# Sums of the input made inside the first down group, and a fifth pair of the up projection by seven products

## The chip, the cores and the metric

The kernel runs on one core of one Trainium2 chip. The metric is the device time of one execution in microseconds, as the median of several runs; smaller is better. The chip's matrix engine is called PE in the profile, its vector engine DVE, its scalar engine ACT, its general engine POOL; SP only issues transfers.

## The reference, cut to what matters

The model is a stack of four layers on 512 tokens with 1024 channels. Each layer has a token mixer (layer 0 and 3 a convolution module, layer 1 neighbourhood attention, layer 2 retention) and after it a gated feed-forward block with a short depthwise convolution. Only the feed-forward block, the channel mixer of the layer, is touched here:

```python
def conv_ffn(h, w_up, dw_w, dw_b, w_down):
    u = dwconv(h @ w_up, dw_w, dw_b)
    val, gate = jnp.split(u, 2, axis=-1)
    return (jax.nn.gelu(gate) * val) @ w_down

for i in range(DEPTH):
    ...
    h = rmsnorm(x, norm2_g[i])
    x = x + conv_ffn(h, ffn_w_up[i], ffn_dw_w[i], ffn_dw_b[i], ffn_w_down[i]).astype(x.dtype)
```

FFN_DIM is 2816, so the up projection has 44 column tiles of 128: 22 of values and 22 of gates. All is float32.

## The kernel before

Everything is kept transposed: a tile has 128 channels as partitions and 512 tokens as columns. Every float32 operand is split into a high and a low part (a cast on ACT makes the high part, a subtraction on DVE the low one), and a product of two such operands takes three matmuls (`mm3`, L184 to L187): high by high, high by low, low by high.

**The up projection.** Pair j of 22 is the value tile j and the gate tile j. In the plain way (`up`, L307) a tile takes 8 channel blocks by 3 matmuls of 512 columns, 24 in all, so a pair takes 48. For the pairs listed in `UPS` (L78) the pair is made at once by Strassen's scheme in Winograd's form, with seven products in place of eight (`up_macro`, L384): the pair is seen as a 2 by 2 block matrix (two output tiles by two halves of the channels) times a 2 by 2 block matrix (two halves of the channels by two halves of the tokens). A product (`uprod`, L371) is 4 blocks by 3 matmuls of 256 columns, so the pair takes 84 matmuls of 256 columns. Two products per pair are left to the start of the next one (`finish_up`). For this scheme there must be sums of the weight blocks and sums of the input blocks. The weight sums of a pair come from `sums` (L484: SP loads a block, POOL adds another to it by an accumulating transfer, tile tag `ws`, three buffers) and `weights` (L501: splits and two additions, on ACT and DVE).

**The input sums.** `combos(p)`, for p from 0 to 3, makes four sums of 256 columns from the normalized input tiles x[2p] and x[2p+1] with four DVE instructions, writes them into one `ws` buffer, and splits them into `ch` (ACT) and `cl` (DVE). `COMBO` (L79) places the four calls behind pairs 4, 5, 6 and 7. The first pair of `UPS` needs all of them.

**Between the matmuls**, `mid` does the depthwise convolution, the GELU and the product of value and gate for a pair, and the sums of that product for the down projection.

**The down projection.** The first 16 blocks of the hidden width are done in two parts (`PARTS`, L71); part 0 starts behind pair 8 (pair 9 in layer 1), part 1 behind pair 16 (17). `down` (L539) runs four groups i = 0 to 3 in each part, each again by seven products of 4 blocks by 3 matmuls of 256 columns. This is what a group does, in the order of the code:

- `weights(...)` for the group;
- product a11 into one half of a PSUM bank, `xc`; ACT copies it to the right half of the tile `s12` (L559);
- product a22 into `v`; then product s2 on top of a11 in `xc`, so it may begin only when that copy has been read;
- ACT copies `xc` again (L562), then s1 and s3;
- ACT takes `xc` into `u2` (L566), DVE subtracts `v` from it (L568), and POOL adds `u2` to the residual in DRAM, `xd[2i]`, by an accumulating transfer (L569);
- the last two products of the group before (`finish`, L541), a DVE addition into its `s12` (L545), and an accumulating transfer of it to `xd[2i+1]` (L546).

The tiles `s12`, `u2` and the temporaries of `mid` share one tag of seven buffers (`NT_FFN`, L75, `t512`). A buffer is used again when its last reader is through; for `s12` and `u2` of a down group that is the transfer by POOL.

**What sets the order.** Each engine runs its own queue in order. The queues are written by a scheduler that goes by its own estimate of durations and by the order of the code; the engines wait for each other by semaphores. A wait holds up everything that stands behind it on its engine. In the names of the waits, DMASW is a transfer issued by POOL that has landed, DMAHW one issued by SP or ACT.

Of the kernel before, what the change touches and what calls it, by code (L numbers as in the profile page):

```python
# [8 lines left out]
F32 = mybir.dt.float32  # L9
F32R = mybir.dt.float32r  # L10
# [7 lines left out]
P = 128  # L18
T = 512
D = 1024  # L20
KD = D // P
DEPTH = 4
EPS = 1e-6
CW = 31
FT = 22
# [49 lines left out]
NT_FFN = 7  # L75
NWS = 3
SCALED = (5, 7, 5, 5)
UPS = ((10, 11, 18, 19), (11, 12, 18, 19), (10, 11, 18, 19), (10, 11, 18, 19))  # L78
COMBO = (4,5,6,7)  # L79
LATEW = True  # L80
COVER = (0, 0)
L1 = 1
SPILL = 2
# [4 lines left out]
def tile_trunk(  # L88
# [9 lines left out]
    const = ctx.enter_context(tc.tile_pool(name="const", bufs=1))  # L98
# [7 lines left out]
    def nm(s):  # L106
        uid[0] += 1
        return f"{s}{uid[0]}"
# [31 lines left out]
    x = [const.tile([P, T], F32, tag=f"x{k}", name=f"x{k}") for k in range(KD)]  # L140
# [53 lines left out]
    def split(src, hi, lo, n=None):  # L194
        state["cast"] = nc.scalar.copy(hi, src)
        return nc.vector.tensor_tensor(lo, src, hi.bitcast(F32), SUB)
# [42 lines left out]
    @contextmanager  # L239
    def behind(*names):  # L240
        with ExitStack() as st:
            for n in names:
                st.enter_context(tc.issue_after(state[n].ins))
            yield
# [57 lines left out]
    def ffn(l, after):  # L302
        with ExitStack() as st:
            stage_pools(st, NT_FFN, 8, 0)
            hp = st.enter_context(tc.tile_pool(name=nm("ffn"), bufs=1, reuse_waits=RW))
# [39 lines left out]
            ch, cl = {}, {}  # L345

            def combos(p):
                e, o = x[2 * p], x[2 * p + 1]
                c = hp.tile([P, D], F32, tag="ws", name=nm("cx"), bufs=NWS)
                q = [c[:, i * 256:(i + 1) * 256] for i in range(4)]  # L350
                with behind("scaled"):
                    nc.vector.tensor_tensor(q[0], e[:, 256:], e[:, :256], SUB)
                    nc.vector.tensor_tensor(q[1], o[:, :256], e[:, :256], SUB)
                nc.vector.scalar_tensor_tensor(q[2], o[:, :256], -1.0, q[0], MUL, SUB)
                nc.vector.scalar_tensor_tensor(q[3], q[2], -1.0, o[:, 256:], MUL, SUB)
                cl[p] = hp.tile([P, D], F32R, tag=f"cl{p}", name=nm("cl"))
                for k, h in ((2 * p, slice(0, T)), (2 * p + 1, slice(T, D))):
                    ch[k] = const.tile([P, T], F32R, tag=f"x{k}", name=nm("ch"))
                    split(c[:, h], ch[k], cl[p][:, h])

            def xblock(p, b):
                if b in (1, 2, 3):
# [138 lines left out]
            def weights(src, r13, sg, r1, hold=False):  # L501
                n = src.shape[-1] // 4
                if r1 is None:
                    r1 = load_raw(src[:, :2 * n], 2 * n)
                w1 = split_w(r1, 2 * n, nc.vector)
                w13 = (whi.tile([P, D], F32R, tag="wh", name=nm("wh")),
                       wlo.tile([P, D], F32R, tag="wl", name=nm("wl")))
                r2 = r13[:, n:2 * n]
                with behind("Hh") if hold else ExitStack():
                    nc.scalar.copy(w13[0][:, :2 * n], r13[:, :2 * n])  # L510
                with behind("Hl") if hold else ExitStack():
                    nc.vector.tensor_tensor(w13[1][:, :2 * n], r13[:, :2 * n],
                                            w13[0][:, :2 * n].bitcast(F32), SUB)
                nc.vector.tensor_tensor(r2, r2, r1[:, :n], ADD)
                h2 = hp.tile([P, T], F32R, tag="h2", name=nm("h2"))
                l2 = hp.tile([P, T], F32R, tag="l2", name=nm("l2"))
                split(r2, h2[:, :n], l2[:, :n])
                nc.vector.tensor_tensor(sg[:, :n], r2, sg[:, n:2 * n], ADD)
                h4 = hp.tile([P, D], F32R, tag="h4", name=nm("h4"))
                l4 = hp.tile([P, D], F32R, tag="l4", name=nm("l4"))  # L520
                split(sg[:, :2 * n], h4[:, :2 * n], l4[:, :2 * n])
                u = lambda w, b: (w[0][:, b * n:(b + 1) * n], w[1][:, b * n:(b + 1) * n])
                return {"a11": u(w1, 0), "a22": u(w1, 1), "s3": u(w13, 0), "s1": u(w13, 1),
                        "s2": u((h2, l2), 0), "sg": u((h4, l4), 0), "a12": u((h4, l4), 1)}

            def down_sums(i, q):
                p0, p1 = PARTS[q]
                c = PART_COL[q]
                return sums(f_down[l, i][:, c:c + 4 * (p1 - p0) * P], state["load"] if i == 0 else None, i == 0)

            def prod(o, w, q, b, start, stop=True, part=None):
                p0, p1 = PARTS[q]
                for p in part or range(p0, p1):
                    s = slice((p - p0) * P, (p - p0 + 1) * P)
                    hi, lo = H[p]
                    mm3(o, w[0][:, s], w[1][:, s], hi[:, b, :], lo[:, b, :],
                        start and p == p0, stop and p == p1 - 1, True)

            def down(q, first, late, filler):  # L539
                p0, p1 = PARTS[q]  # L540

                def finish(i, w, v, s12):
                    prod(v[:, :256], w["sg"], q, 2, False)
                    prod(v[:, 256:], w["a12"], q, 3, True)
                    nc.vector.tensor_tensor(s12, v, s12, ADD)  # L545
                    nc.gpsimd.dma_start(xd[2 * i + 1], s12, accum_op=ADD)  # L546

                prev = None
                for i in range(4):
                    w = weights(*down_sums(i, q)) if i else first  # L550
                    xb, v = bank(psa), bank(psa)
                    xc = xb[:, :256]
                    s12 = t512()
                    if i == 0:
                        prod(xc, w["a11"], q, 1, True, part=range(p0, p1 - 1))
                        prod(v[:, 256:], w["a22"], q, 6, True, part=range(p0, p1 - 1))
                    now = range(p1 - 1, p1) if i == 0 else None
                    prod(xc, w["a11"], q, 1, True, part=now)
                    nc.scalar.copy(s12[:, 256:], xc)  # L559
                    prod(v[:, 256:], w["a22"], q, 6, True, part=now)  # L560
                    prod(xc, w["s2"], q, 0, False)
                    nc.scalar.copy(s12[:, :256], xc)  # L562
                    prod(v[:, :256], w["s1"], q, 4, True)
                    prod(xc, w["s3"], q, 5, False)
                    u2 = t512()
                    nc.scalar.activation(u2.rearrange("p (h t) -> p h t", h=2),  # L566
                                         xc.unsqueeze(1).broadcast_to([P, 2, 256]), AF.Copy, scale=-1.0)
                    nc.vector.tensor_tensor(u2, u2, v, SUB)  # L568
                    nc.gpsimd.dma_start(xd[2 * i], u2, accum_op=ADD)  # L569
                    if prev:  # L570
                        finish(*prev)
                    prev = (i, w, v, s12)
                late()
                filler()
                finish(*prev)
# [49 lines left out]
            def fetch_sums(j):  # L625
                if j in UPS[l] and j not in ahead:
                    ahead[j] = sums(f_us[l, UPS[l].index(j)], state["load"])

            def ups_of(j):
                nonlocal n  # L630
                fetch_sums(j + 1)
                if j in UPS[l] and n < 2 * j + 2:
                    ups.extend(up_macro(j))
# [5 lines left out]
                for p in range(4):  # L639
                    if COMBO[p] == j:  # L640
                        combos(p)

            starts = {2 * p1 + (l == 1 and q == 0) * L1 + COVER[q]: q for q, (_, p1) in enumerate(PARTS)}
            for j in range(1, FT):
                ups_of(j)
                w0 = down_sums(0, starts[j]) if j in starts else None
                if w0 and not LATEW:
                    w0 = weights(*w0)
                if n > S2[l]:
                    mids(j)  # L650
                if w0 and LATEW:
                    w0 = weights(*w0, True)
# [690 lines left out]
    kind, l = seq[0]  # L1343
# [51 lines left out]
def _layout(inp):  # L1395
    import numpy as np

    f = {k: np.asarray(v) for k, v in inp.items()}
# [12 lines left out]
    par = np.zeros((P, NPAR), np.float32)  # L1411
# [25 lines left out]
    cl = np.arange(16)[:, None, None, None]  # L1437
    kc = np.arange(32)[None, None, :, None]
    masks = []
    for b, ks in ((0, 0), (1, 8), (3, 32)):  # L1440
        c = 16 * b + cl
# [10 lines left out]
    for sh in range(PH):  # L1452
        for r in range(PH):
# [12 lines left out]
    fu = f["ffn_w_up"].reshape(4, 4, 2, P, 44, P)  # L1466
    fus = np.stack([np.stack([np.concatenate(
        [fu[l, :, par, :, j + c].transpose(1, 0, 2).reshape(P, T)
         for c, par in ((0, 0), (FT, 1), (FT, 0), (0, 1))], -1) for j in UPS[l]]) for l in range(DEPTH)])
    fd = f["ffn_w_down"].reshape(4, FT, P, 8, P)  # L1470
    macros = []
    for i in range(4):
# [48 lines left out]
```

## Time and profile before

| what | us |
|---|---|
| median of 3 runs | 2527.53 |
| lowest and highest run | 2527.3 and 2529.24 |
| the profiled execution, whole | 2528.47 |
| its span in the trace | 2526.7 |
| busy in that span: DVE | 1825.3 (72%) |
| busy in that span: ACT | 1267.8 (50%) |
| busy in that span: POOL | 373.0 (15%) |

The profiled execution is 1.77 us longer than its span, and 0.94 us longer than the median of the runs. Starts are counted from the beginning of the span. [...]

### The profile page before, as it was taken

The page shows a single profiled execution, that of the slowest core. Times are in us where ns is not written, and L with a number is a line of the kernel's source. Part 1 is how long each engine was busy: PE and PEld are TensorE (multiplying, and loading weights), DVE is VectorE, ACT ScalarE, POOL GpSimd, SP SyncE. Part 2 cuts the span into 40 slices and gives each one's busy share as a digit, 9 for nine tenths or more (in the row PEclk, how much of TensorE's full clock was granted, in tenths as well). Part 3 has the DMA queues.
Part 4 walks back from the last instruction along what each step waited for, and adds up shares of the span by engine and source line. Part 5 has one row for each costly group of instructions (what it writes and reads, how often), then busy time and mean ns, then how long its engine had stood idle before and what let it go on. Part 6 is the DMA issues. An engine that isn't in the chain of part 4 may idle for free.

```text
span 2526.7 us, 38769 instructions
## 1 busy us (share of the span) xinstructions
PE 2508.2 (99%) x15166; PEld 2170.0 (86%) x15166; DVE 1825.3 (72%) x3021; ACT 1267.8 (50%) x1778; POOL 373.0 (15%) x443
## 2 busy tenths in 40 slices
PE   9999999999999999999999999999999999999999
PEld 7888898989998889898888888889898888789897
DVE  7976867677877786767656566686767887686765
ACT  5454645465656565555332423464545445464543
POOL 2114010103320201120000000201010121201010
PEclk9999999999999999999999999999999999999999
DMA  7736776746653566773222222477664673477664
GB/s 257 227 96 184 192 162 176 164 141 163 141 136 109 138 169 165 195 172 116 75 84 74 83 75 65 145 185 162 175 163 142 206 228 89 121 193 162 177 161 133
DMA packets 130153, 379.22 MB, mean 150 GB/s; under 512 B 15360, under 2 KB 22400, under 8 KB 129968
## 3 DMA queue, kind: packets, MB, share of 16 engines
q1 hardware_dynamic: 90816, 280.45, 35.5%
q0 software_dynamic: 38000, 93.96, 20.1%
q8 instruction: 119, 1.95, 0.3%
q10 hardware_dynamic: 1152, 2.33, 0.3%
q14 instruction: 66, 0.54, 0.1%
HBM read 342.11 MB, written 30.79 MB: 148 GB/s over the span
## 4 chain that ended last, share of the span: by engine, by line
PE 93%; issue 3%; DVE 2%; DMA 1%; ACT 1%; SPq 0%; POOL 0%; DVEq 0%; POOLq 0%; ACTq 0%
PE ps L185 22%; PE ps L186 22%; PE ps L187 22%; PE ps L320 3%; PE ps L315 3%; PE ps L316 3%; PE ps L190 3%; PE ps L192 3%; PE ps L191 3%; PE ps L778 1%; PE ps L777 1%; PE ps L776 1%; DMA wl<-in_f_up 1%; PE ps L472 1%; PE ps L473 1%
## 5 line engine op out<-in xcount | busy, mean ns | idle before, releaser
L171 ACT CAST wh<-wr 128x1024 fp32r<-128x1024 f32 (+1 forms) x311 | 318.5, 1027 | 552.6 <-PE ps L186 317.7
L186 PE MATMUL ps<-xl,wh 128*128 128x512 f32 (+1 forms) x1256 | 489.7, 390 | 0.3 <-DVE xl L257 0.3
L187 PE MATMUL ps<-xh,wl 128*128 128x512 f32 (+1 forms) x1256 | 489.2, 390 | 0.1
L185 PE MATMUL ps<-xh,wh 128*128 128x512 f32 (+1 forms) x1256 | 488.3, 390 | 0.8 <-ACT wh L171 0.8
L172 DVE TENSOR_TENSOR wl<-wr,wh 128x1024 fp32r<-128x1024 f32 (+1 forms) x308 | 372.1, 1209 | 142.4 <-ACT wh L171 131.1
L185 PEld LDWEIGHTS ps<-xh,wh 128*128 128x128 f32 x1256 | 235.9, 188 | 54.9 <-ACT wh L171 1.7
L187 PEld LDWEIGHTS ps<-xh,wl 128*128 128x128 f32 x1256 | 235.8, 188 | 52.9 <-DVE wl L172 0.5
L186 PEld LDWEIGHTS ps<-xl,wh 128*128 128x128 f32 x1256 | 236.0, 188 | 52.6 <-DVE xl L257 0.6
L186 PE MATMUL ps<-Hl,wh 128*128 128x256 f32 (+1 forms) x734 | 224.1, 307 | 0.0
L185 PE MATMUL ps<-Hh,wh 128*128 128x256 f32 (+1 forms) x734 | 221.6, 308 | 0.0
L187 PE MATMUL ps<-Hh,wl 128*128 128x256 f32 (+1 forms) x734 | 221.2, 307 | 0.0
L315 PE MATMUL ps<-xh,wh 128*128 128x512 f32 x408 | 161.6, 396 | 0.0
L316 PE MATMUL ps<-xl,wh 128*128 128x512 f32 x408 | 161.0, 395 | 0.0
L190 PE MATMUL ps<-wh,xh 128*128 128x256 f32 (+1 forms) x512 | 159.0, 313 | 0.8 <-ACT xh L254 0.8
L192 PE MATMUL ps<-wh,xl 128*128 128x256 f32 (+1 forms) x512 | 159.1, 311 | 0.0
L191 PE MATMUL ps<-wl,xh 128*128 128x256 f32 (+1 forms) x512 | 159.0, 312 | 0.0
L185 PEld LDWEIGHTS ps<-Hh,wh 128*128 128x128 f32 x734 | 138.4, 189 | 11.4 <-ACT wh L171 4.3
L186 PEld LDWEIGHTS ps<-Hl,wh 128*128 128x128 f32 x734 | 138.1, 188 | 7.2
L187 PEld LDWEIGHTS ps<-Hh,wl 128*128 128x128 f32 x734 | 137.1, 188 | 7.1
L181 POOL DMA_DIRECT2D wl<-in_f_up x51 | 44.6, 874 | 461.7 <-ACT wl L180 369.3
L185 PE MATMUL ps<-Hh,h 128*128 128x256 f32 x384 | 108.5, 282 | 0.0
L186 PE MATMUL ps<-Hl,h 128*128 128x256 f32 x384 | 108.5, 282 | 0.0
(330 smaller groups left out, 6151.4 us busy)
## 6 DMA issues: line engine op xcount, KB each, us to landing
wr<-in_f_up SPq DMA_DIRECT2D x144, 512.0 KB, 4.3
wraw<-in_cdw SPq DMA_DIRECT2D x56, 608.0 KB, 5.3
wl<-in_f_up POOLq DMA_DIRECT2D x51, 512.0 KB, 7.8
wr<-in_f_down SPq DMA_DIRECT2D x32, 512.0 KB, 5.9
ws<-in_f_down SPq DMA_DIRECT2D x32, 512.0 KB, 7.9
ws<-in_f_down POOLq DMA_DIRECT2D x32, 512.0 KB, 8.3
xd<-t POOLq DMA_DIRECT2D x64, 256.0 KB, 7.8
wr<-in_cw_in SPq DMA_DIRECT2D x30, 512.0 KB, 4.2
```

The lines of the kernel that those rows point to most:

```text
L171: nc.scalar.copy(hi[:, :n], raw[:, :n])
L172: eng.tensor_tensor(lo[:, :n], raw[:, :n], hi[:, :n].bitcast(F32), SUB)
L181: nc.gpsimd.dma_start(lo[:, :n], src.bitcast(F32R), accum_op=ADD)
L185: nc.tensor.matmul(o, wh, ah, start=first, stop=False, skip_group_check=free)
L186: nc.tensor.matmul(o, wh, al, start=False, stop=False, skip_group_check=free)
L187: nc.tensor.matmul(o, wl, ah, start=False, stop=last, skip_group_check=free)
L190: nc.tensor.matmul(o, ah, wh, start=first, stop=False)
L191: nc.tensor.matmul(o, ah, wl, start=False, stop=False)
L192: nc.tensor.matmul(o, al, wh, start=False, stop=last)
L315: nc.tensor.matmul(ps, wh[:, s], xhi[k], start=k == 0, stop=False)
L316: nc.tensor.matmul(ps, wh[:, s], xlo[k], start=False, stop=False)
L320: nc.tensor.matmul(ps, wl[:, k * P:(k + 1) * P], xhi[k], start=False, stop=k == KD - 1)
```

## The change

Two things are changed. Pair 12 joins the list of pairs that are made by seven products, in layers 0, 2 and 3; layer 1 had it before and keeps four such pairs. And the four calls of `combos` move from behind pairs 4 to 7 into the first part of the down projection in all four layers: `combos(i)` is called in group i, behind the `finish` of the group before. The sums are now held in two tiles of the seven-buffer tag and no more in a `ws` buffer.

```diff
-UPS = ((10, 11, 18, 19), (11, 12, 18, 19), (10, 11, 18, 19), (10, 11, 18, 19))
-COMBO = (4,5,6,7)
+UPS = ((10, 11, 12, 18, 19), (11, 12, 18, 19), (10, 11, 12, 18, 19), (10, 11, 12, 18, 19))
+COMBO = (99,99,99,99)
 LATEW = True
+INGROUP = True
...
             def combos(p):
                 e, o = x[2 * p], x[2 * p + 1]
-                c = hp.tile([P, D], F32, tag="ws", name=nm("cx"), bufs=NWS)
-                q = [c[:, i * 256:(i + 1) * 256] for i in range(4)]
+                c = [t512(), t512()]
+                q = [c[i // 2][:, i % 2 * 256:i % 2 * 256 + 256] for i in range(4)]
...
-                for k, h in ((2 * p, slice(0, T)), (2 * p + 1, slice(T, D))):
-                    ch[k] = const.tile([P, T], F32R, tag=f"x{k}", name=nm("ch"))
-                    split(c[:, h], ch[k], cl[p][:, h])
+                for i in range(2):
+                    ch[2 * p + i] = const.tile([P, T], F32R, tag=f"x{2 * p + i}", name=nm("ch"))
+                    split(c[i], ch[2 * p + i], cl[p][:, i * T:(i + 1) * T])
...
                     if prev:
                         finish(*prev)
+                    if INGROUP and q == 0:
+                        combos(i)
                     prev = (i, w, v, s12)
```

(The layout of the weights on the host is filled up to five pairs for every layer.) Lines behind L80 stand one lower in the changed kernel, and behind the call of `combos` three.

On ACT, in layer 0 before the change, this stands where the third and the fourth group of the first part begin: `t466` and `t481` are their `s12`, `t452` and `t467` the `u2` of the second and the third group, `h4` and `h2` parts of the weight sums.

```order
L566 ACTIVATE t452_3486<-ps449_3421 128x512 [waits PE_49]
L559 COPY t466_3543<-ps464_3541 128x256
L195 CAST h4447_3417<-wq439_3397 128x1024 [waits DMAHW1_49,PE_49]
L171 CAST wh490_3775<-wr489_3773 128x1024 [waits DMAHW0_49,DVE_49,PE_49]
L195 CAST h2475_3652<-ws468_3636 128x512 [waits DVE_49,PE_49,Activation_49]
L562 COPY t466_3543<-ps464_3541 128x256 [waits PE_49]
L171 CAST wh494_3806<-wr493_3804 128x1024 [waits DMAHW2_49,PE_49]
L566 ACTIVATE t467_3606<-ps464_3541 128x512 [waits PE_49]
L559 COPY t481_3663<-ps479_3661 128x256
L195 CAST h4462_3537<-wq454_3517 128x1024 [waits DMAHW7_49,DVE_49,PE_49]
```

The same place in the changed kernel, where `t460` and `t480` are the `s12` of the third and the fourth group, and `t441` and `t461` the `u2` of the second and the third:

```order
L567 ACTIVATE t441_3451<-ps438_3386 128x512 [waits PE_49]
L560 COPY t460_3521<-ps458_3519 128x256 [waits DMASW5_49,Activation_49]
L196 CAST ch445_3488<-t442_3481 128x512 [waits DVE_49]
L196 CAST h4436_3382<-wq428_3362 128x1024 [waits DMAHW1_49,PE_49]
L196 CAST ch446_3491<-t443_3482 128x512 [waits DVE_49]
L172 CAST wh494_3779<-wr493_3777 128x1024 [waits DMAHW0_49,PE_49,Activation_49]
L196 CAST h2474_3643<-ws467_3627 128x512 [waits DVE_49,PE_49,Activation_49]
L563 COPY t460_3521<-ps458_3519 128x256 [waits PE_49]
L172 CAST wh498_3810<-wr497_3808 128x1024 [waits DMAHW2_49,PE_49]
L567 ACTIVATE t461_3584<-ps458_3519 128x512 [waits PE_49]
L560 COPY t480_3654<-ps478_3652 128x256 [waits DMASW0_49,Activation_49]
L196 CAST ch465_3621<-t462_3614 128x512 [waits DVE_49]
```

The two copies now wait for a transfer of POOL. In the built program `t460` has the address of `t421`, the `u2` of the first group, and DMASW5 is the transfer of it to `xd[0]`; `t480` has the address of `t441`, and DMASW0 is the transfer of that to `xd[2]`. In the same way the second tile of sums of the third and the fourth `combos`, written by DVE, waits for the transfers to `xd[1]` and `xd[4]`, and the `s12` of pair 10 for that to `xd[6]`. The casts of `ch` stand between the copies now.

On PE this is where the fourth group of the changed kernel goes on with `xc` (`ps478`); `ps492` is an ordinary tile of pair 9.

```order
L186 MATMUL ps492_3776<-xh4_91,wh494_3779 128x512
L187 MATMUL ps492_3776<-xl4_99,wh494_3779 128x512
L188 MATMUL ps492_3776<-xh4_91,wl495_3780 128x512
L186 MATMUL ps492_3776<-xh5_92,wh494_3779 128x512
L186 MATMUL ps478_3652<-Hh335_2780,h2474_3643 128x256 [waits Activation_49]
L187 MATMUL ps478_3652<-Hl336_2781,h2474_3643 128x256
L188 MATMUL ps478_3652<-Hh335_2780,l2475_3644 128x256 [waits DVE_49]
```

The count of the semaphore of ACT for which the first matmul of product s2 waits is that of the copy into `t480`. In every layer this matmul is number 281 of the first part: 280 matmuls stand ahead of it from the first product of the part on, 264 of 256 columns and 16 of 512. Before the change it was number 290 in layer 0.

On DVE, in layer 0 before the change, this stands from the third group's weights to the low part of the third group's sum `ws453`, whose buffer the weight sums of pair 11 take next:

```order
L172 TENSOR_TENSOR wl457_3524<-wr455_3521,wh456_3523 128x1024 [waits DMAHW4_49,PE_49,Activation_49]
L512 TENSOR_TENSOR wl459_3528<-ws453_3516,wh458_3527 128x1024 [waits DMASW2_49,DMAHW2_49,PE_49,Activation_49]
L568 TENSOR_TENSOR t437_3392<-t437_3392,ps435_3328 128x512 [waits Activation_49]
L514 TENSOR_TENSOR ws453_3516<-ws453_3516,wr455_3521 128x512 [waits DVE_49]
L518 TENSOR_TENSOR wq454_3517<-ws453_3516,wq454_3517 128x512 [waits DMAHW7_49,DVE_49]
L172 TENSOR_TENSOR wl472_3644<-wr470_3641,wh471_3643 128x1024 [waits DMAHW5_49,PE_49,Activation_49]
L196 TENSOR_TENSOR l2461_3533<-ws453_3516,h2460_3532 128x512 [waits PE_49,Activation_49]
```

And in the changed kernel, where that sum is `ws447` and `t422` and `t423` hold the sums of `combos(0)`:

```order
L353 TENSOR_TENSOR t422_3348<-x0_79 128x256
L354 TENSOR_TENSOR t422_3348<-x1_80,x0_79 128x256
L355 SCALAR_TENSOR_TENSOR t423_3349<-x1_80,t422_3348 128x256 [waits DVE_49]
L513 TENSOR_TENSOR wl453_3506<-ws447_3494,wh452_3505 128x1024 [waits DMASW2_49,DMAHW2_49,PE_49,Activation_49]
L356 SCALAR_TENSOR_TENSOR t423_3349<-t423_3349,x1_80 128x256 [waits DVE_49]
L569 TENSOR_TENSOR t421_3344<-t421_3344,ps419_3280 128x512 [waits Activation_49]
L197 TENSOR_TENSOR cl424_3354<-t422_3348,ch425_3355 128x512 [waits Activation_49]
L515 TENSOR_TENSOR ws447_3494<-ws447_3494,wr449_3499 128x512 [waits DVE_49]
L173 TENSOR_TENSOR wl471_3635<-wr469_3632,wh470_3634 128x1024 [waits DMAHW5_49,PE_49,Activation_49]
L197 TENSOR_TENSOR cl424_3354<-t423_3349,ch426_3358 128x512 [waits Activation_49]
L519 TENSOR_TENSOR wq448_3495<-ws447_3494,wq448_3495 128x512 [waits DMAHW7_49,DVE_49]
L197 TENSOR_TENSOR l2455_3511<-ws447_3494,h2454_3510 128x512 [waits PE_49,Activation_49]
```

Six instructions of `combos(0)` have come in ahead of the last reader of that buffer. On POOL the transfers of this place keep their order up to the fifth: to `xd[0]`, the accumulation for pair 11 (L498, which needs that buffer), to `xd[1]`, to `xd[2]`; behind them now come `xd[4]`, the accumulation for pair 12, and `xd[3]`, `xd[6]`, `xd[5]`, `xd[7]`. Outside the feed-forward blocks the order is as it was, but for two neighbouring rows of DVE in the last layer's convolution.

More of the change, by code (lines that the diff above doesn't have):

```diff
@@ L1468, in _layout @@
         [fu[l, :, par, :, j + c].transpose(1, 0, 2).reshape(P, T)
-         for c, par in ((0, 0), (FT, 1), (FT, 0), (0, 1))], -1) for j in UPS[l]]) for l in range(DEPTH)])
+         for c, par in ((0, 0), (FT, 1), (FT, 0), (0, 1))], -1) for j in (2 * UPS[l])[:max(map(len, UPS))]]) for l in range(DEPTH)])
     fd = f["ffn_w_down"].reshape(4, FT, P, 8, P)
```

## The prediction

> **What bounds the kernel now.** I read the page first: the busy shares and the shares of the chain that ended last.
>
> ```profile
> span 2526.7 us, 38769 instructions
> PE 2508.2 (99%) x15166; PEld 2170.0 (86%) x15166; DVE 1825.3 (72%) x3021; ACT 1267.8 (50%) x1778; POOL 373.0 (15%) x443
> PE 93%; issue 3%; DVE 2%; DMA 1%; ACT 1%; SPq 0%; POOL 0%; DVEq 0%; POOLq 0%; ACTq 0%
> ```
>
> PE is the bound. Work taken from PE shortens the time, and any moment in which PE must wait lengthens it; work of the others is free while it stays beside PE. Next come the stages that the change touches: the last plain pair ahead of the first down part of layer 0, and groups two to four of that part (each stretch with PE, PEld, DVE, ACT and POOL busy in us).
>
> ```profile
> 298.00:309.60 11.60, 11.60 (x52) 9.32 (x51) 10.74 (x15) 4.89 (x7) 0.44 (x1) 1.00 0.75 176
> 321.00:331.50 10.50, 10.50 (x91) 10.50 (x90) 4.94 (x7) 4.43 (x7) 1.76 (x2) 1.00 0.81 185
> 331.50:342.00 10.50, 10.50 (x89) 10.41 (x88) 5.92 (x7) 4.96 (x8) 2.67 (x3) 1.00 0.86 205
> 342.00:352.60 10.60, 10.60 (x69) 9.54 (x69) 6.08 (x7) 4.14 (x7) 1.73 (x2) 1.00 0.99 214
> ```
>
> PE is busy in every microsecond at the full granted clock (1.00), in the pairs and in the down groups. DVE is nearly full in the pair (10.74 of 11.60) and half idle in the groups (4.94 to 6.08 of 10.5). The DMA engines are the reverse of idle there: 0.81 to 0.99. So the groups have room on DVE, and PE has no gap that the move could close: taking `combos` away from pairs 4 to 7 gains nothing. What can be gained is PE's own work.
>
> **The gain.** What a matmul costs is the distance of starts; these are the rows of PE at the edge of the two stages.
>
> ```profile
> 299.79 0.40 PE L186 MATMUL ps<-xl,wh 128*128 128x512 f32 x1
> ...
> 309.59 0.40 PE L186 MATMUL ps<-xl,wh 128*128 128x512 f32 x1
> ...
> 310.06 0.28 PE L185 MATMUL ps<-Hh,wh 128*128 128x256 f32 x1
> ...
> 314.33 0.28 PE L185 MATMUL ps<-Hh,wh 128*128 128x256 f32 x1
> ```
>
> Between the first two lie 42 matmuls of 512 columns: 9.80 / 42 = 0.2333 us each. Between the last two lie 36 of 256 columns: 4.27 / 36 = 0.1186 us. A plain pair is 48 x 0.2333 = 11.20 us of PE, a pair by seven products 84 x 0.1186 = 9.96 us. Pair 12 saves 1.24 us in each of three layers, **3.7 us** in all. Layer 1 has no such saving.
>
> **The new waits.** In each group `combos` takes two of the seven buffers in which `s12` and `u2` live, so the `s12` of the third group comes into the buffer of the first group's `u2`, and that of the fourth into that of the second group's `u2`. Each such copy on ACT now waits until POOL's accumulating transfer out of the old tile has landed. Before, the fourth group's `u2` was the first to wait for such a landing, late enough to cost nothing. These are the two copies before, then POOL's transfers `xd[0]`, the accumulation for pair 11, `xd[1]`, `xd[2]`, then the landing times of `xd[0]`, `xd[1]` and `xd[2]`, each asked for alone.
>
> ```profile
> 332.27 0.36 ACT L559 COPY t<-ps 128x256 f32<-128x256 f32 x1
> 342.51 0.36 ACT L559 COPY t<-ps 128x256 f32<-128x256 f32 x1
> ...
> 326.30 1.23 POOL L569 DMA_DIRECT2D xd<-t  x1
> 335.76 0.87 POOL L497 DMA_DIRECT2D ws<-in_f_us  x1 [8.24 <-DVE l L196]
> 336.30 1.23 POOL L546 DMA_DIRECT2D xd<-t  x1
> 336.85 1.59 POOL L569 DMA_DIRECT2D xd<-t  x1
> ...
> DMA to landing us min/median/max: 8.1/8.1/8.1
> DMA to landing us min/median/max: 10.0/10.0/10.0
> DMA to landing us min/median/max: 10.7/10.7/10.7
> ```
>
> `xd[0]` lands at 326.30 + 8.1 = 334.4 and `xd[2]` at 336.85 + 10.7 = 347.55, 2.1 and 5.0 us behind the starts of the copies before. ACT stands still that long, with the casts of `ch` and of the weight sums `h4` queued behind the copy. What counts is when PE asks. By the order of the changed kernel the product s2 of the third group stands behind 206 matmuls of 256 columns, 24.43 us from the first product of the part, and that of the fourth behind 264 of 256 and 16 of 512 columns: 264 x 0.1186 + 16 x 0.2333 = 35.04 us. In layer 0 the part begins at 310.06, so PE asks at 334.49 and 345.10. The third group's copy (0.36 us) is ready at 334.8: 0.3 us lost, which the later wait swallows, since that one hangs on an absolute time. The fourth group's copy is ready at 347.55 + 0.36 = 347.91, so PE loses 2.8 us. The start of the part and `xd[2]` in layers 1, 2 and 3:
>
> ```profile
> 931.45 0.28 PE L185 MATMUL ps<-Hh,wh 128*128 128x256 f32 x1
> 1709.18 0.28 PE L185 MATMUL ps<-Hh,wh 128*128 128x256 f32 x1
> 2267.80 0.28 PE L185 MATMUL ps<-Hh,wh 128*128 128x256 f32 x1
> ...
> L569 POOL DMA_DIRECT2D xd<-t x1: 1222/1222/1222, 957.6 to 957.6; - x1
> DMA to landing us min/median/max: 10.0/10.0/10.0
> ...
> L569 POOL DMA_DIRECT2D xd<-t x1: 1351/1351/1351, 1737.7 to 1737.7; - x1
> DMA to landing us min/median/max: 10.5/10.5/10.5
> ...
> L569 POOL DMA_DIRECT2D xd<-t x1: 1347/1347/1347, 2295.3 to 2295.3; - x1
> DMA to landing us min/median/max: 13.2/13.2/13.2
> ```
>
> With 35.04 us from the start and 0.36 us for the copy, PE would wait 967.6 + 0.36 - 966.49 = 1.5 us in layer 1, 1748.2 + 0.36 - 1744.22 = 4.3 us in layer 2 and 2308.5 + 0.36 - 2302.84 = 6.0 us in layer 3. Together with layer 0: **14.6 us**.
>
> **The transfers start later as well.** POOL takes its transfers in order, and `xd[2]` stands behind the accumulation for pair 11, which waits for SP's load into the buffer whose last reader is a subtraction on DVE (`l<-ws`, at 326.83).
>
> ```profile
> 319.77 1.23 DVE L172 TENSOR_TENSOR wl<-wr,wh 128x1024 fp32r<-128x1024 f32 x1 [1.11 <-ACT wh L171]
> 322.63 1.22 DVE L512 TENSOR_TENSOR wl<-ws,wh 128x1024 fp32r<-128x1024 f32 x1 [1.63 <-ACT wh L510]
> ...
> 326.83 0.69 DVE L196 TENSOR_TENSOR l<-ws,h 128x512 fp32r<-128x512 f32 x1
> ...
> L352 DVE TENSOR_TENSOR cx<-x x16: 412/416/418, 241.6 to 2218.5; 128x256 f32<-128x256 f32 x16
> L196 DVE TENSOR_TENSOR cl<-cx,ch x32: 674/682/689, 246.9 to 2231.4; 128x512 fp32r<-128x512 f32 x32
> ```
>
> In the changed kernel the six instructions of `combos(0)` stand ahead of that reader: 4 x 0.42 + 2 x 0.68 = 3.0 us. Three of the short ones fit into the hole of 1.63 us ahead of 322.63; of the rest little is covered, since DVE runs on without a gap from there to 326.83. The delay lies between 0 and 3.0 us; I take 3.0 less the hole, about 1.5, as nothing but that hole hides them. In four layers: **6.0 us** (0 to 12).
>
> **Behind the stall** another ring stands: `combos(2)` waits on DVE for `xd[1]`, so the third `u2` and `xd[4]` go out later; `combos(3)` waits for `xd[4]`, the fourth `u2` stands behind it, and the `s12` of pair 10 waits for its transfer `xd[6]`. In layer 0: `xd[1]` at 336.30 + 10.0 + 1.5 = 347.8, DVE 2 us, `xd[4]` alone in the queue 4.2 us (row below), DVE 3 us, `xd[6]` behind other transfers 8.1: 365.1. PE comes there 74 matmuls of 256 and 32 of 512 columns (16.2 us) behind its stall, at 349.4 + 16.2 = 365.6. I take 0; with 8.1 us for `xd[4]` too it is 3.4 us a layer, 14 in all, the upper end.
>
> **The sum** against the profiled execution: 2528.47 - 3.7 + 14.6 + 6.0 = 2545.4 us. The median of the runs is 0.94 lower: **2544.5 us**, 0.67% slower.
>
> **Rivals.**
>
> *The landings come in time* (not slower). All that stalls PE is the time of `xd[2]`. Started at 336.85 + 1.5, it would have to land by 345.10 - 0.36 = 344.7, within 6.4 us. Alone in its queue a transfer of this size can do that:
>
> ```profile
> L546 POOL DMA_DIRECT2D xd<-t x1: 862/862/862, 352.8 to 352.8; - x1
> DMA to landing us min/median/max: 4.2/4.2/4.2
> ```
>
> Then the saving alone is left: 2527.53 - 3.7 = 2523.8, which is within 0.2%, about what a measurement of this kernel can tell from no change. For it speaks that layer 1 is only 1.5 us late. Against it: in all four layers `xd[2]` took 10.0 to 13.2 us behind a transfer of twice its size and `xd[1]`, with the DMA engines at 0.86 to 0.99, and POOL's order keeps those ahead of it. 17%. [...]
>
> *The second ring closes too.* If `xd[4]` takes 8.1 us as `xd[0]` did, 14 us come on top: 2558. For it speaks that the DMA engines are nearly full in that stretch (0.99); against it that the order now lets `xd[4]` go ahead of `xd[3]`. 12%.
>
> *DVE becomes the bound in three pairs by seven products in a row.* Two in a row before:
>
> ```profile
> 362.70:389.00 26.30, 26.30 (x180) 24.26 (x179) 18.18 (x23) 16.05 (x22) 1.76 (x2) 1.00 0.41 111
> ```
>
> DVE was busy 18.18 of 26.30 us there, 9.1 us for a pair against 9.96 of PE. For pair 12 the change brings three splits of 1024 columns (1.22 each, as at 322.63) and five additions or splits of 512 (0.69, as at 326.83), 7.1 us, in place of one split of 1.2. If none of these 5.9 us were covered in three layers, and no landing late, it is 2523.8 + 17.7 = 2541.5. The 8.1 us idle in that row are against it. 5%.
>
> **Chances and range.** Forecast 64%, landings in time 17%, second ring 12%, DVE 5%, 2% for what I don't see. The forecast's own range is 2536 to 2553: the delay of 0 to 3.0 us a layer moves it by 6 either way, and a few microseconds of the second ring come on top. The range reaches down to the first rival, 2523.5, and up to 2555. Faster by over 0.2% would be below 2522.5, more than the whole saving: 6%, for a saving in landings and order that I overlooked. Within 0.2%: 19%, the first rival and forecasts whose stalls come to less than 9 us. Slower: 75%.
>
> **What would show it.** PE's gaps in the changed trace: one of 1.5 to 8 us in each layer some 35 us behind the first matmul on `Hh`, ended by ACT's copy L560, with ACT idle just before that copy and released by a transfer `xd<-t`. If `xd[2]` still takes 10 us but no gap stands there, the count of PE's rows is wrong; if it takes under 6, the queue is. Pair 12 should take 84 starts at 0.1186 us. A gap at the first products s2 of pair 10 would be the second ring; gaps ended by DVE in pairs 10 to 13 the third rival. PE without gaps and a span near 2523 would make the whole prediction wrong.

## The result, and the profile after

| | before | after |
|---|---|---|
| median of six runs each, us | 2528.38 | 2543.52 |
| lowest and highest run, us | 2527.30 and 2531.48 | 2541.85 and 2545.63 |
| profiled execution, us | 2528.47 | 2542.55 |

The ratio is 1.0060, with a 95% interval of 1.0050 to 1.0071: slower, by 15 us. The forecast of 2544.5 us lies 1.0 us above the measured median; it stood 17.0 us above its own base of 2527.53 us, where the measured medians lie 15.1 us apart. How it comes to that is another matter, as the trace shows.

The page of the changed kernel, first the span and the busy times, then the chain that ended last by engine, then the group of matmuls to which product s2 of the down groups belongs (busy, mean ns of one, idle time ahead of them):

```profile
span 2540.8 us, 39036 instructions
...
PE 2511.1 (99%) x15274; PEld 2177.2 (86%) x15274; DVE 1844.0 (73%) x3042; ACT 1272.7 (50%) x1790; POOL 373.2 (15%) x443
...
PE 93%; DMA 3%; DVE 2%; ACT 1%; issue 1%; POOL 0%; SPq 0%; DVEq 0%; POOLq 0%; ACTq 0%
...
L186 PE MATMUL ps<-Hh,h 128*128 128x256 f32 x384 | 110.7, 288 | 11.3 <-ACT t L560 11.3
```

DMA has risen from 1% to 3% of the chain, and this one group of matmuls has 11.3 us of idle time ahead of it, all of it ended by ACT's copy L560. What released that copy is in the answer for its line:

```profile
its engine sat idle before it (us, times) until:
  DMA xd<-t: 31.2, 8
  PE ps L188: 10.8, 8
who waited for it (us, times):
  PEld ps L186: 13.0, 4
  PE ps L186: 11.3, 4
```

Eight copies, two in each layer, wait for a transfer `xd<-t`, and four of them make PE wait. This is PE in layer 0 at that place:

```profile
345.18 0.40 PE L186 MATMUL ps<-xh,wh 128*128 128x512 f32 x1
348.20 0.39 PE L186 MATMUL ps<-Hh,h 128*128 128x256 f32 x1 [2.62 <-ACT t L560]
348.42 0.28 PE L187 MATMUL ps<-Hl,h 128*128 128x256 f32 x1
...
349.25 0.33 PE L188 MATMUL ps<-Hh,l 128*128 128x256 f32 x1
349.38 0.41 PE L186 MATMUL ps<-Hh,h 128*128 128x256 f32 x1
349.59 0.41 PE L187 MATMUL ps<-Hl,h 128*128 128x256 f32 x1
...
350.44 0.63 PE L187 MATMUL ps<-xl,wh 128*128 128x512 f32 x1
350.87 0.63 PE L188 MATMUL ps<-xh,wl 128*128 128x512 f32 x1
```

The gap is the one that was forecast, 35 us behind the start of the part (310.22 here). But there is more: from 349.38 on, starts of 256 columns stand 0.21 us apart in place of 0.1186, and those of 512 columns 0.43 in place of 0.2333. The windows of this stretch say why (PE, PEld, DVE, ACT, POOL busy; then the granted clock of PE, the share of the DMA engines, GB/s):

```profile
346.00:348.00 2.00, 0.00 (x0) 0.00 (x0) 1.82 (x3) 0.22 (x1) 0.00 (x0) 1.00 0.98 220
348.00:350.00 2.00, 1.80 (x12) 1.80 (x13) 1.97 (x5) 2.00 (x4) 0.86 (x1) 0.84 0.92 186
350.00:352.00 2.00, 2.00 (x8) 1.71 (x7) 1.73 (x2) 0.51 (x2) 0.99 (x2) 0.50 1.06 246
352.00:354.00 2.00, 2.00 (x8) 1.58 (x8) 0.00 (x0) 0.63 (x1) 0.78 (x1) 0.81 1.04 201
```

The granted clock falls to 0.50 some 1 us behind the end of the gap and stays there for 3.4 us. The column of PE's busy time hides it: PE is busy 2.00 of 2.00 us, at half speed. The same in the four layers, from the starts of PE (a gap is the distance of two starts less that of a full stream; slow starts are what the starts behind it lose up to 17 us later), with `xd[2]` from its rows on POOL:

| layer | `xd[2]` issued behind the start of the part, before and after | to landing, before and after | gap at s2 | slow starts |
|---|---|---|---|---|
| 0 | 26.79, 26.70 | 10.7, 10.8 | 2.79 | 1.63 |
| 1 | 26.20, 26.59 | 10.0, 10.7 | 2.59 | 1.64 |
| 2 | 28.55, 26.76 | 10.5, 11.0 | 2.76 | 1.63 |
| 3 | 27.54, 26.67 | 13.2, 11.8 | 3.78 | 2.82 |

Gaps of 11.9 us and slow starts of 7.7 us, 19.6 together. From the start of the first down part to that of the second, the four layers take 16.3 us longer in all, so some 3.3 us of the 19.6 are made up there, near the saving of 3.7. The span is 14.1 longer, because the stretch between the parts of layers 2 and 3 is 2.1 us shorter: a gap of 1.92 us in the convolution of layer 3 had half-speed starts behind it in this profile of before (2.0 us lost) and hardly any in that of after (0.4 us). The last 0.1 us is the balance of smaller differences.

### The profile page after: what moved, and what is told of

It is laid out like the page before. It is cut to its first block, busy times and chain, and to the rows that moved or that the text cites. A ratio compares the mean times of both kernels' runs of the same rounds, so it can differ in the third digit from the quotient of the medians.

```text
span 2540.8 us, 39036 instructions
## 1 busy us (share of the span) xinstructions
PE 2511.1 (99%) x15274; PEld 2177.2 (86%) x15274; DVE 1844.0 (73%) x3042; ACT 1272.7 (50%) x1790; POOL 373.2 (15%) x443
## 4 chain that ended last, share of the span: by engine, by line
PE 93%; DMA 3%; DVE 2%; ACT 1%; issue 1%; POOL 0%; SPq 0%; DVEq 0%; POOLq 0%; ACTq 0%
PE ps L186 22%; PE ps L187 22%; PE ps L188 22%; PE ps L321 4%; PE ps L316 4%; PE ps L317 4%; PE ps L193 3%; PE ps L192 3%; PE ps L191 3%; DMA xd<-t 2%; PE ps L781 1%; PE ps L780 1%; PE ps L779 1%; DMA ws<-in_f_us 1%; PE ps L473 1%
## 5 line engine op out<-in xcount | busy, mean ns | idle before, releaser
L186 PE MATMUL ps<-xh,wh 128*128 128x512 f32 (+1 forms) x1244 | 483.0, 389 | 1.1 <-ACT wh L172 1.1
L316 PE MATMUL ps<-xh,wh 128*128 128x512 f32 x384 | 152.1, 396 | 0.0
L317 PE MATMUL ps<-xl,wh 128*128 128x512 f32 x384 | 151.5, 395 | 0.0
L186 PE MATMUL ps<-Hh,h 128*128 128x256 f32 x384 | 110.7, 288 | 11.3 <-ACT t L560 11.3
L188 PE MATMUL ps<-Hh,l 128*128 128x256 f32 x384 | 109.9, 286 | 0.0
```

The lines of the kernel that those rows point to most:

```text
L186: nc.tensor.matmul(o, wh, ah, start=first, stop=False, skip_group_check=free)
L188: nc.tensor.matmul(o, wl, ah, start=False, stop=last, skip_group_check=free)
L316: nc.tensor.matmul(ps, wh[:, s], xhi[k], start=k == 0, stop=False)
L317: nc.tensor.matmul(ps, wh[:, s], xlo[k], start=False, stop=False)
```

## The experiments

Ratios are to the kernel before, run beside each on the same chip.

### 1. The sums in another tile, in three layers of four

```diff
-                c = [t512(), t512()]
+                if l == 1:
+                    c = [t512(), t512()]
+                else:
+                    f = hp.tile([P, 7, 256], F32, tag="F", name=nm("F")).rearrange("p a b -> p (a b)")
+                    c = [f[:, :T], f[:, T:2 * T]]
```

> The changed kernel, but in layers 0, 2 and 3 the sums of the input lie in the tile F of 7 x 256 columns (free during the first down part) in place of two of the seven buffers; layer 1 is left as it is and is the control. So in three layers the copies into the third and fourth s12 no longer wait for a transfer. Theory (the wait for xd[2] stalls PE, and the low granted clock behind it is caused by the stall): the gap before the fourth group's s2 and the slow starts behind it go together in layers 0, 2 and 3 (4.4 + 4.7 + 6.6 = 15.7 us) and stay in layer 1 (2.6 us of gap and 1.6 us of slow starts): 2543.5 - 15.7 = 2527.8 us. Rival A (the slow starts have another cause, such as the full DMA engines at that time): only the gaps go (2.8 + 2.8 + 3.8 = 9.4 us): 2534.1 us, with starts 0.21 us apart still there. Rival B (it is the place of the calls, DVE or the order that costs the time): nothing changes, 2543.5 us within 2.

Measured: ratio 1.0008 (0.9999 to 1.0017), span 2530.0 us. In layers 0, 2 and 3 the copies wait for no transfer, and gap and slow starts are gone together; layer 1, the control, keeps an idle time of 2.63 us and slow starts of 1.6. So it is the wait that costs, and here the low clock follows from it. Of the 15.7 us, 3.7 come back at the same place in smaller gaps (0.9, 1.6 and 1.2 us), such as this one in layer 0: DVE now makes the low parts late.

```profile
349.68 0.39 PE L188 MATMUL ps<-Hh,l 128*128 128x256 f32 x1 [0.62 <-DVE l L197]
```

### 2. One transfer put behind another on POOL

The buffers and their waits stay, and so does the whole order of PE and of ACT, row for row. On POOL the accumulation for the second pair moves (and in layers 0, 2 and 3 the one for pair 12 changes places with the transfer behind it); on DVE four rows a layer change places, some 34 to 38 us behind the start of the part.

```diff
-                    nc.gpsimd.dma_start(r13[:, :2 * n], src[:, :2 * n], accum_op=ADD)
+                    with tc.issue_after(late.ins) if late else ExitStack():
+                        nc.gpsimd.dma_start(r13[:, :2 * n], src[:, :2 * n], accum_op=ADD)
...
-                    nc.gpsimd.dma_start(xd[2 * i], u2, accum_op=ADD)
+                    t = nc.gpsimd.dma_start(xd[2 * i], u2, accum_op=ADD)
+                    if i == 1:
+                        state["xd2"] = t
...
-                    ahead[j] = sums(f_us[l, UPS[l].index(j)], state["load"])
+                    ahead[j] = sums(f_us[l, UPS[l].index(j)], state["load"], False,
+                                    state["xd2"] if UPS[l].index(j) == 1 else None)
```

> The changed kernel with one transfer moved on POOL: the accumulation for the second pair by seven products (11, in layer 1: 12) is issued behind xd[2] in place of ahead of xd[1]. Nothing else is changed, the buffers and their waits stay. Theory (what stalls PE is the time at which xd[2] lands, and that is set by what is ahead of it in POOL's queue): xd[2] goes out when DVE has made u2, some 24.3 us behind the start of the part in place of 26.7, behind xd[1] alone; with 4.2 to 9 us to landing it is there before PE asks (35.0 us), no gap, no slow starts: 2543.5 - 20.0 = 2523.5 us; if it still takes 10.8 us, a gap of 0.5 us a layer without slow starts: 2525.5 us. Rival (the transfers queue by bytes on the DMA engines whatever their order): landing where it was, gap where it was, 2543.5 us within 2.

> The changed kernel with the accumulation for the second pair by seven products behind xd[2], once more with more rounds. Theory (it keeps the saving of 3.7 us and loses 2 us less in gaps than nothing: 1.1 + 0.5 + 0.6 us are left): 2526.7 us of span before - 4.2 = 2522.5, a ratio of 0.9983. Rival (the saving is taken back where the profile doesn't show it): a ratio of 1.000 or more.

Measured: 0.9993 (0.9984 to 1.0003), and with more rounds 0.9984 (0.9975 to 0.9993), medians of 2525.45 and 2525.06 us. The theory holds. This is the one version that beats both kernels, if only just: the interval of the first measurement still reaches no change. POOL in layer 0 of the first of these runs, the transfers to `xd[1]` and `xd[2]` and then the accumulation:

```profile
332.35 0.87 POOL L548 DMA_DIRECT2D xd<-t  x1 [6.56 <-DVE t L547]
333.28 0.86 POOL L571 DMA_DIRECT2D xd<-t  x1
334.82 0.87 POOL L499 DMA_DIRECT2D ws<-in_f_us  x1 [0.68 <-DMA ws<-in_f_us]
```

The answer for the second of them alone:

```profile
DMA to landing us min/median/max: 4.8/4.8/4.8
```

The part began at 308.81, so `xd[2]` goes out 24.47 us behind it and lands in 4.8 us (in the other layers 8.0, 6.4 and 6.9) in place of 10.8. No gap is left at s2 of the fourth group, and no slow starts. What remains are 0.5 to 1.1 us a layer in three layers, in the first of the runs. In the profile of the second, 2.1 us of idle time stand at s2 of the third group, whose copy waits for `xd[0]` (0.7 us in layer 0, 1.5 in layer 2). The DMA engines are as full as in the windows above, and the clock stays up:

```profile
342.00:344.00 2.00, 2.00 (x10) 1.60 (x9) 0.47 (x1) 1.47 (x2) 0.86 (x1) 1.00 1.05 395
```

### 3. Without pair 12, with and without that order

`UPS` is set back to four pairs in the changed kernel and in the kernel of experiment 2.

> The changed kernel without pair 12: only the input sums are moved into the down groups. Theory: the saving of 3.7 us is missing and the stalls stay: 2543.5 + 3.7 = 2547.2 us, a gap of 2.4 to 3.8 us before the fourth group's s2 in all four layers with some 1.6 to 2.8 us of slow starts behind it. Rival (pair 12, by its own transfers and its load on DVE, makes the landing late): the gaps shrink and the time falls below 2543 us.

> The same without pair 12 (four pairs by seven products, moved input sums, the accumulation behind xd[2]). Theory (moving the sums gains nothing by itself, and the saving of pair 12 is 3 x 1.24 us once no landing is waited for): 3.7 us above the kernel with five pairs, a span of 2526.2 us, ratio 1.000 to before. Rival (the move itself gains by freeing DVE in the pairs ahead of the part): within 1 us of the kernel with five pairs.

Measured: 1.0070 (1.0055 to 1.0085) and 1.0002 (0.9993 to 1.0010). The first is 0.0010, or 2.5 us, above the changed kernel's ratio (the intervals overlap), where 3.7 were expected: in two layers gaps of 2.5 to 2.6 us had hardly any slow starts behind them. Layer 0:

```profile
347.64 0.39 PE L186 MATMUL ps<-Hh,h 128*128 128x256 f32 x1 [2.42 <-ACT t L560]
347.87 0.28 PE L187 MATMUL ps<-Hl,h 128*128 128x256 f32 x1
...
349.06 0.28 PE L188 MATMUL ps<-Hh,l 128*128 128x256 f32 x1
349.17 0.33 PE L186 MATMUL ps<-Hh,h 128*128 128x256 f32 x1
349.33 0.28 PE L187 MATMUL ps<-Hl,h 128*128 128x256 f32 x1
```

The second prices pair 12: 2528.56 against 2525.06 us on the same chip, 3.5 us for three pairs, where 3.7 was worked out; by the two intervals the 3.5 is uncertain by about 3 us. And moving the sums gains nothing by itself: without the stall, with four pairs, the time is that of the kernel before.

### 4. The fifth pair without the move

> The kernel before with pair 12 by seven products in layers 0, 2 and 3, the input sums left behind pairs 4 to 7 in their ws buffer. Theory (the saving of 3 x 1.24 us is whole, all of the loss comes from the move into the first down part): 2528.4 - 3.7 = 2524.7 us, pair 12 as 84 starts at 0.1186 us, no gap over 1 us that the kernel before doesn't have. Rival (three pairs by seven products in a row make DVE the bound): gaps ended by DVE or ACT in pairs 10 to 13, up to 2541 us.

The edit is the new `UPS` in the kernel before. Measured: 1.0012 (1.0003 to 1.0022), span 2529.1 us. The theory falls here: the fifth pair alone gains nothing, and is slower by 0.0003 to 0.0022. PE lost 2.8, 1.9 and 2.1 us in layers 0, 2 and 3 in the second down part, most of it at its start. Who waited for whom at that place in layer 2 (us, times, longest):

```profile
ACT Hh L195 <- DVE F L437: 3.4, 1, 3.4
PEld ps L185 <- ACT wh L171: 1.0, 1, 1.0
PE ps L185 <- ACT wh L171: 0.8, 1, 0.8
```

The last products of value and gate for that part (`F`, L437) are late on DVE; the casts of `Hh` wait for them, the casts of the part's weights stand behind those on ACT, and PE waits for these. It is the chain of my third rival, at a place that I had not named. DVE was not full: 45.3 of the 58 us ahead of the part, against 48.0 in experiment 2. So I take it to be the order in which its work came; that is argued, and why this order is worse was not tried. But the two changes belong together: with the same five pairs and the input sums moved, PE loses nothing at that place, neither in the changed kernel nor in experiment 2. Alone, the move gains nothing (experiment 3) and the fifth pair gains nothing; together, without the stall, they gain.

### 5. More pairs

A sixth pair in the kernel of experiment 2: pair 13, and in another run pair 20. Pair 20 also as the fifth pair in the kernel before.

> The same with pair 13 by seven products as well in all four layers. Theory (PE is the bound and DVE keeps up): 4 x 1.24 = 5.0 us below the kernel with five pairs, a span of 2517.5 us, ratio 0.9964. Rival (DVE falls behind in a longer row of such pairs, as in the run with the fifth pair only, where the last sums for the second down part came late): gaps at the start of the second part of 1 to 3 us a layer, a time between 2519 and 2530 us.

> The changed kernel with the accumulation for the second pair behind xd[2], and pair 20 by seven products too in all four layers. Theory: 4 x 1.24 = 5.0 us below the kernel without it, a span of some 2518 to 2520 us, ratio 0.9965. Rival (three such pairs in a row behind the second part make DVE or the weight sums late there, as six in a row did ahead of it): gaps behind pair 18, ratio 0.9985 or more.

> The kernel before with pair 20 in place of pair 12 as the fifth pair by seven products in layers 0, 2 and 3, the input sums left behind pairs 4 to 7. Theory (with pair 12 only, the loss of 6.8 us came because the last sums for the second part, which starts behind pair 16, were made late on DVE; pair 20 lies behind that start): no gaps at the start of the second part, the saving of 3.7 us is whole: a span of 2523.0 us, ratio 0.9985. Rival (any fifth pair loses by its own weight sums and transfers): gaps near pair 20 or at the end of the layer, ratio 1.000 or more.

Measured: 1.0078 (1.0065 to 1.0090), 1.0126 (1.0109 to 1.0143) and 1.0103 (1.0088 to 1.0118). All three go to the rivals, and further than they said. With pair 13, PE loses 6 to 7 us a layer in the second down part, by the chain of experiment 4. With pair 20 it is one gap of 6.2 us near the end of each layer in which the pair was added; in layer 0 of the last run the matmul behind it takes 0.79 us, where those of 512 columns ahead of it took 0.39 or 0.40:

```profile
544.64 0.79 PE L185 MATMUL ps<-Hh,wh 128*128 128x512 f32 x1 [6.23 <-ACT Hh L195]
```

The remaining blocks of the down projection need the hidden values of the last pairs, which come from `mid` on DVE and ACT. A pair that is shorter on PE brings that need closer, and its own sums put DVE's work off; this is an argument, and no run separates the two. (The expectation speaks of six such pairs in a row ahead of the second part; the kernel with pair 13 has four, 10 to 13, in layers 0, 2 and 3, and three in layer 1.)

### 6. Two runs that missed their aim

> The kernel before, but in the fourth group of the first down part ACT makes the first copy of xc into s12 13, 15, 17 and 20 times over (layers 0, 1, 2, 3), with the same data each time. Product s2 then waits for the last copy, with no transfer in it. In layer 0 the copy began at 342.51 and PE asked at 347.2; at 0.37 to 0.42 us a copy the gaps come to 0.5 to 1.5, 1 to 2, 1.5 to 3 and 2.5 to 4 us. Theory (the length of the idle time alone brings the granted clock down): no slow starts behind the short gaps, and behind those over some 2.5 us starts 0.213 us apart for 3 us and more, which costs 1.4 to 2.8 us on top of the gap. Rival (the low clock comes with the landing transfers or the full DMA engines): starts 0.1186 us apart behind every one of the gaps.

```diff
-                    nc.scalar.copy(s12[:, 256:], xc)
+                    for _ in range(DOSE[l] if i == 3 and q == 0 else 1):
+                        nc.scalar.copy(s12[:, 256:], xc)
```

One run of 2528.78 us beside 2528.96, and no gap at s2: the scheduler knows what a copy takes and put s2 34 places further back on PE. This says nothing on the clock.

> The kernel with the accumulation for the second pair behind xd[2], and with 2, 3, 4 and 5 extra transfers (layers 0, 1, 2, 3) ahead of xd[2] in POOL's queue, each writing the same 256 KB of u2 to scratch memory. Theory (PE's loss is set by the landing of xd[2], and the granted clock falls behind a gap of more than some 2.5 us): each extra transfer takes POOL 1.2 us to issue and puts the landing off by 1.2 to 3 us; without them xd[2] landed 29.3 to 32.6 us behind the start of the part, and the copy must begin by 34.6. So a gap of 0 to 1 us in layer 0, growing by 1 to 3 us a layer to some 3 to 8 us in layer 3; starts 0.21 us apart only behind the gaps over 2.5 us, for 3 us or more. Rival A (the slow starts come with the number of transfers under way): slow starts in all layers, also without a gap. Rival B (the landing isn't what PE waits for): no gap that grows with the number, and a time within 3 us of 2525.

```diff
+                    for k in range(DOSE[l] if i == 1 and q == 0 else 0):
+                        t = nc.gpsimd.dma_start(scr[k], u2)
```

One run of 2529.32 us beside 2527.99. The extra transfers cost POOL 0.55 us each and no more (`xd[2]` went out 25.6 to 27.3 us behind the start and landed in 6.3 to 9.2), so they made no dose; no gap at s2 grew with them. But in layer 3 another wait closed, by chance: the `s12` of pair 10 waited for `xd[6]`, the second ring of the prediction. ACT, then PE, then the windows:

```profile
2319.69 0.37 ACT L393 COPY t<-ps 128x256 f32<-128x256 f32 x1 [3.91 <-DMA xd<-t]
```

```profile
2317.73 0.27 PE L188 MATMUL ps<-xl,wh 128*128 128x256 f32 x1
2320.11 0.38 PE L187 MATMUL ps<-ch,h 128*128 128x256 f32 x1 [2.11 <-ACT t L393]
...
2321.09 0.42 PE L188 MATMUL ps<-Hl,h 128*128 128x256 f32 x1
2321.31 0.42 PE L189 MATMUL ps<-Hh,l 128*128 128x256 f32 x1
```

```profile
2320.00:2322.00 2.00, 1.89 (x12) 1.89 (x13) 1.14 (x2) 0.59 (x2) 0.00 (x0) 0.74 0.39 130
2322.00:2324.00 2.00, 2.00 (x11) 2.00 (x11) 0.00 (x0) 0.00 (x0) 0.00 (x0) 0.50 0.00 0
```

The clock is at 0.50 while the DMA engines move nothing (0.00), and in experiment 2 it was at 1.00 while they were full (1.05). With pair 13 it fell in layer 0 at a place where PE stood still for more than half of the time and the DMA engines were at 0.00 and 0.01:

```profile
436.00:438.00 2.00, 0.75 (x6) 0.54 (x5) 1.97 (x3) 0.68 (x1) 0.00 (x0) 1.00 0.01 2
438.00:440.00 2.00, 0.98 (x3) 0.69 (x3) 1.97 (x6) 1.65 (x4) 0.00 (x0) 0.75 0.00 0
440.00:442.00 2.00, 1.34 (x6) 1.14 (x5) 2.00 (x3) 1.81 (x3) 0.00 (x0) 0.50 0.00 0
```

So in these runs the low clock went with PE's idle time and not with the transfers.

## Why the prediction was right, and where it was not

- **The saving** of 3 x 1.24 us: right in this kernel. The time from the first down part to the second, less the gap and the slow starts, fell from 127.17 to 125.95 us in layer 0, 1.22 us; experiment 3 measured 3.5 us for all three. But it hangs on the move of the sums, which the prediction held to gain nothing: without the move the fifth pair gains nothing (experiment 4).
- **The new wait**: right in place, cause and form. The copy that was named, at the matmul that was named, in all four layers, released by `xd[2]`. The sum of the prediction, with the issue and the landing that were measured, gives the gaps: in layer 0, 26.70 + 10.8 + 0.36 - 35.04 = 2.82 us against 2.79; in layer 3, 26.67 + 11.8 + 0.36 - 35.04 = 3.79 against 3.78; in the other two it is within 0.35. That 14.6 us were forecast and 11.9 found comes mostly from the issue: `xd[2]` left 1.8 us sooner behind the start in layer 2 and 0.9 in layer 3, 0.4 later in layer 1. The landings cancel (0.1, 0.7 and 0.5 us longer in layers 0, 1 and 2, 1.4 shorter in layer 3). The 0.3 us at the third group did not come: `xd[0]` landed 22.6 us behind the start in layer 0, where 24.3 were worked out. In experiments 2 and 3 that wait does close in some layers. Experiments 1 and 2 took the wait away by the buffer and by the queue, and each time the gap and the slow starts went with it.
- **The transfers start later**, 6.0 us: wrong. The step that failed is that a later reader means a later transfer. The reader `l<-ws` did come 1.46 us later behind the start of the part (18.23 in place of 16.77), as was worked out, and SP's load with it. But the load then landed sooner. These are the loads for pair 11 in layer 0, after and before:

```profile
L495 SPq DMA_DIRECT2D ws<-in_f_us x1: 379/379/379, 329.2 to 329.2; - x1
...
DMA to landing us min/median/max: 6.1/6.1/6.1
```

```profile
L494 SPq DMA_DIRECT2D ws<-in_f_us x1: 379/379/379, 327.5 to 327.5; - x1
...
DMA to landing us min/median/max: 7.7/7.7/7.7
```

  So in layer 0 the accumulation and the two transfers behind it left when they had left before, and `xd[2]` 0.6 us sooner in the mean of the four layers. The term is nothing or slightly below.
- **What a stall costs**: wrong, and in the other direction. I priced a wait at its length. Behind the gaps PE ran at half the clock (0.50) for 3.4 us in layers 0 to 2 and for 6.1 us in layer 3, which cost 7.7 us in the four. The sum came out within 1 us of the median because this missing term is about as large as what the false one added and the gaps fell short. That they cancel is chance. The trace of before could have warned me. It has a wait in the convolution of layer 0, and the windows there show the same fall of the clock behind it:

```profile
133.13 0.52 PE L753 MATMUL ps<-ident,t 128*128 128x128 f32 x3 [1.93 <-DVE t L747]
```

```profile
131.00:133.00 2.00, 0.20 (x1) 0.00 (x0) 1.76 (x4) 1.59 (x2) 0.00 (x0) 1.00 0.43 165
133.00:135.00 2.00, 1.87 (x22) 1.90 (x23) 2.00 (x3) 0.59 (x1) 0.52 (x1) 0.79 0.07 13
135.00:137.00 2.00, 2.00 (x22) 2.00 (x21) 0.33 (x1) 0.40 (x1) 1.74 (x4) 0.50 0.71 113
```

- **The landings in time** did not happen, but experiment 2 is that rival made true, at 2525.1 to 2525.5 us where 2523.8 was worked out for it. A transfer of these 256 KB took 4.2 us with nothing ahead of it (before), 4.8 to 8.0 behind one other of its size (experiment 2), and 10.7 to 11.8 behind that and one of twice the size (changed kernel).
- **The second ring** stayed open in the changed kernel; no gap stands at pair 10's s2. It is close, though: it closed in one layer of one other run.
- **DVE as the bound** in pairs 10 to 13: not in the changed kernel, where those pairs have no gap. Experiments 4 and 5 show a variant of it, work of DVE and ACT that is late where the down projection needs it, in each further kernel with another pair: pair 12 without the move, pair 13 and pair 20.
- **The range**: the 6 us either way that the prediction names give 2538.5 to 2550.5; the 2536 at its lower end does not follow from them. Nothing hangs on it.

## What to carry to other kernels

A buffer ring that is shortened turns a transfer's landing into a wait: count how long the old reader has until the buffer comes round, on the queue that it is in, before tiles are added to a ring. If such a wait closes, look at the order of the queue first; here moving one transfer behind another was worth 0.0076 of the time, some 19 us, five times what the fifth pair saves. And price a stall of the matrix engine at more than its length: of nine between 2.36 and 3.89 us here, seven had a half-speed stretch behind them that cost 1.4 to 2.8 us more (next section).

## What was not expected of the hardware

**The clock behind short stalls.** The profiles of the changed kernel and of experiments 1 and 3 hold nine idle times of PE between 2.36 and 3.89 us at s2. Behind seven of them PE fell to half the clock and lost 1.4 to 2.8 us by it. Behind one of 2.36 and one of 2.42 us it lost next to nothing, yet it fell behind one of 2.11 (experiment 6) and one of 1.93 (before). So the length of one gap does not decide alone. The idle time of 2.42 us is that of layer 0 in experiment 3, whose rows stand there; the clock (third number from the end) stays up behind it:

```profile
345.00:347.00 2.00, 0.22 (x1) 0.00 (x0) 2.00 (x4) 0.00 (x0) 0.00 (x0) 1.00 0.79 239
347.00:349.00 2.00, 1.36 (x11) 1.36 (x12) 1.78 (x4) 1.78 (x4) 0.86 (x1) 1.00 0.51 106
349.00:351.00 2.00, 2.00 (x12) 1.73 (x12) 2.00 (x3) 0.85 (x3) 0.86 (x1) 1.00 0.98 192
```

Layer 1 of the changed kernel has an idle time of the same 2.42 us, from 970.58 to 973.01, and there the clock is at 0.50 from 973.99 to 977.40:

```profile
971.00:973.00 2.00, 0.00 (x0) 0.00 (x0) 2.00 (x3) 0.42 (x2) 0.00 (x0) 1.00 0.43 81
973.00:975.00 2.00, 1.99 (x13) 2.00 (x14) 1.93 (x5) 1.94 (x3) 0.86 (x1) 0.75 0.68 236
975.00:977.00 2.00, 2.00 (x7) 1.71 (x7) 1.54 (x2) 0.37 (x1) 0.86 (x1) 0.50 1.06 143
977.00:979.00 2.00, 2.00 (x9) 1.58 (x8) 0.00 (x0) 0.82 (x1) 0.00 (x0) 0.90 0.93 142
```

The gap of 1.93 us in the convolution of layer 0, and its like in layer 3, stand in the profiles of both kernels, at 1.92 or 1.93 us each. Behind three of these four the clock was at 0.50 for 3.4 us; behind that of layer 3 in the changed kernel, from 2098.96 to 2100.88, it stayed at 1.00, and the first 50 starts behind it took 3.21 us where they took 4.71 before. So a stall of the same length cost 1.5 us more in one profile than in the other. What decides whether the clock falls was not shown by these runs.

**The same load took less time when it was issued later**, and by more than the change had put it off: in layer 0 it landed in 6.1 us when it was issued 1.5 us later, and in 7.7 before. In the four layers it went out 1.0 to 1.5 us later behind the start of the part and took 1.1 to 3.1 us less; why was not tested. So here a later load was no delay for what waits for it.
